# Attention with a bias on one core: the first transposes, copies and casts in another order over the engines, and a planner with other times

## The chip, the cores and the metric

One core of a Trainium2 chip. The metric is the device time of one launch in microseconds (us); the median of the runs counts. The engines: PE (TensorE, matmuls and transposes), DVE (VectorE), ACT (ScalarE), POOL (GpSimd, which here casts a little and issues loads) and SP (which issues transfers). Each takes its own instructions in order; they wait for each other by semaphores.

## The reference

Softmax attention over 4 x 8 heads of 1024 positions and 64 dimensions, with one bias matrix for all heads:

```
scores = q @ k^T / 8 + bias          # 1024 x 1024 per head
attn   = exp(scores - max) / (sum(exp(scores - max)) + 1e-8)
out    = attn @ v                    # float32
```

The kernel leaves the maximum out (the scores are small) and gets the sum as a 65th column of the product with V, which holds ones.

## The kernel before

**Tiling.** Heads go in pairs (16 pairs). The 1024 queries are cut into eight chunks of 128, and these into three passes: A has the chunks 6 and 7, B 3 to 5, C 0 to 2. Pairs go in three groups (0 to 3, 4 to 8, 9 to 15), whose passes run in the order ABC, CAB and BCA. A pass, a pair and a head make a step; a step has two *slots*, so there are 192 slots. A slot is half of the keys against the chunks of the pass and fills two banks of PSUM (512 float32 columns of 128 partitions each) in pass A and three in B and C. Even slots lie in the tile `sx`, odd ones in `sy`.

**What a slot goes through.** PE fills its banks (`s_fill`, L151): the scores come on top of what the banks held. Only the first step of a pass in a group is a *restart*, which clears the banks and adds the bias by matmuls with `btraw`, the bias in bf16. In every later step the product of K (`KA`, `KB`) with Q (`QA`, `QB`) is built so that it takes the scores of the step before away and adds those of the new one; so a bank is never cleared, but PE cannot fill slot s + 2 before slot s has been read. ACT then takes the exponential of the banks into `E` in SBUF (`s_exp`, L202). In marked slots the last bank goes to DVE: L216 takes it out of PSUM (`d_fixed`), and a chain of six further instructions (`d_steps`, L228 to L233) makes the exponential of it by polynomials, into a tile `e`. PE multiplies `E` or `e` with V (`VV`) into `po` (L265); a *unit*, four slots, is divided by its sums and written out by DVE (`evac`, L276 and L277), through three buffers `ob` and SP's queue (L278).

**K and Q** come through POOL's queue in float32 and are cast on the way to bf16 (`kr`, `qr`), are transposed by PE into a PSUM tile `px` of one of two tags, `xa` and `xb` (which the `po` of the units share), and copied by DVE into `KA`, `KB`, `QA` and `QB`; later pairs get some copies by transfers on SP's queue.

**The prologue** (L289 to L487) does the slots 0 to 5 by hand, in the order in which the code is written. The first K, Q and bias chunks come as float32 through the queues of SP and ACT into a part of `E` and are cast by engines, which DVE, ACT and POOL share (L340 to L376 and further); POOL's own loads follow its casts in its queue. The first pair is transposed and scored in halves: `pk` are the transposes of the first head's K, `pq` and `pq_` those of Q, `pk0` the second head's K, `pk1` and `pq1` the second pair. `scores`, `bias_` and `exp_` issue the matmuls of a half and its exponential. A load marked by `after` waits for another's landing.

**The planner** (L490 to L987) emits the rest. It keeps a clock for ACT, PE and DVE and takes whatever could start next by its own costs (L490: 427 for a bank of exponential and so on, in ns). It starts from a state that is written out by hand: when the slots of the prologue end (`act_end`, `fill_end`), when `xa` and `xb` come free (`x_free`), when operands are there (`R`), and when raw K and Q (`raw_at`), V (`v_ready`) and the bias parts land. Its constants set which slots are marked for DVE (`DMIN`, `DTAIL`, the last slots are left out, and `REM`, the work that may be outstanding), how far PE may delay a fill for transposes (`PSL`, `PSU`, `URG`), how many blocks of `E` may wait (`RING`) and behind which slot a load is issued (`G0` to `G5`). Its clock decides only the order; on the chip each instruction waits for what it needs.

Of the kernel before, what the change touches and what calls it, by code (L numbers as in the profile page):

```python
# [9 lines left out]
BF = mybir.dt.bfloat16  # L10
# [6 lines left out]
def kernel(  # L17
# [11 lines left out]
    nc = tc.nc  # L29
    B, H, S, D = q.shape  # L30
    P = 128
    NCH = S // P
# [5 lines left out]
    kf = k.rearrange("b (g t) (p c) d -> (b g) p t (c d)", t=2, p=P)  # L38
# [13 lines left out]
    ps = ctx.enter_context(tc.tile_pool(name="ps", bufs=1, space=bass.MemoryType.PSUM))  # L52

    ident = consts.tile([P, P], BF)
# [4 lines left out]
    btraw = consts.tile([P, NCH, S], BF)  # L59
    KA = consts.tile([P, RP, NCH * P], BF)  # L60
    KB = consts.tile([P, RP, NCH * P], BF)
    QA = consts.tile([P, RP, NCH * P], BF)
    QB = consts.tile([P, RP, NCH * P], BF)
# [61 lines left out]
    raws = {}  # L125
# [11 lines left out]
    def transpose_pe(px, src, c0, n):  # L137
        for c in range(n):
            for t in range(2):
                nc.tensor.transpose(px[t * D:(t + 1) * D, c, :], src[:, t, c0 + c, :], ident[:])  # L140
# [140 lines left out]
    with tc.manual_schedule():  # L281

        def cast(eng, dst, src):
            if eng is nc.scalar:
                eng.copy(dst, src)
            else:
                eng.tensor_copy(dst, src)

        sq0, sk0, sk0b = stage(256), stage(512), stage(512)  # L289
        sc = {6: stage(1024), 7: stage(1024)}  # L290
        sk1, sq1 = stage(1024), stage(256)
# [8 lines left out]
        behind = sp_.dma_start(out=sk0b, in_=kf[0][:, 1])  # L300
# [5 lines left out]
        g, v_, sc_ = nc.gpsimd, nc.vector, nc.vector.tensor_scalar  # L306
# [17 lines left out]
        def q_part(pr, c0, c1, src):  # L324
            return raws[pr, 0][:, :, c0:c1, :], src.rearrange("p (t c d) -> p t c d", t=2, d=D)

        def load_q(pr, c0, c1):
            return g.dma_start(out=raws[pr, 0][:, :, c0:c1, :].rearrange("p t c d -> p t (c d)"),
                               in_=qf[pr][:, :, c0 * D:c1 * D])

        HK = S // 2
        kr0, qr0, kr1, qr1 = raws[0, 1], raws[0, 0], raws[1, 1], raws[1, 0]
        sync = mybir.DependencyInfo(mybir.DependencyClass.Sync, mybir.DependencyReason.SCHED_ONLY)

        def after(later, earlier):

            tc.add_manual_dep(later.ins, earlier.ins.name, sync, reason="pace of the loads")


        cast(g, btraw[:, 6, 5 * P:], sc[6][:, 5 * P:])  # L340
        for pr in (2, 3):
            if pr == 3:
                cast(g, kr1[:, 1].rearrange("p c d -> p (c d)"), sk1[:, 512:])
                load_q(pr, 6, 8)
            x = g.dma_start(out=raws[pr, 1].rearrange("p t c d -> p t (c d)"), in_=kf[pr])
            if pr == 2:
                after(x, behind)
            if pr == 2:
                cast(g, btraw[:, 7, HK:], sc[7][:, HK:])
                load_q(pr, 6, 8)  # L350
        load_q(0, 0, 6)
        g.dma_start(out=btraw[:, 3:6, :], in_=bf_[:, 3:6, :])
        load_v(0)
# [9 lines left out]
        def on(y, lo, hi, inst):  # L363
            for y2, lo2, hi2, x in used:
                if y2 == y and (hi2 <= lo or hi <= lo2):
                    apart(inst, x)
            used.append((y, lo, hi, inst))
            return inst
# [7 lines left out]
        cast(v_, *q_part(0, 6, 8, sq0))  # L376

        pk = [XY[y][:, 1024:1024 + 2 * P].bitcast(BF) for y in range(2)]
        for c in range(NCH):
            on(c // 4, 2, 3, nc.tensor.transpose(pk[c // 4][:D, c % 4 * P:(c % 4 + 1) * P], kr0[:, 0, c, :], ident[:]))  # L380
        pq = ps.tile([P, 2, P], BF, tag="xa", name="px")
        pq_ = ps.tile([P, 2, P], BF, tag="xb", name="px")
        for c in range(2):
            nc.tensor.transpose(pq_[:D, c, :], qr0[:, 0, 6 + c, :], ident[:])
        transpose_pe(pq, qr0, 6, 2)
        on(0, 2, 3, nc.scalar.copy(KA[:D, 0, :HK], pk[0][:D]))
        on(1, 2, 3, v_.tensor_copy(KA[:D, 0, HK:], pk[1][:D]))
        v_.tensor_copy(QB[:D, 0, 6 * P:], pq_[:D].rearrange("p c q -> p (c q)"))
        nc.scalar.copy(btraw[:, 6, :5 * P], sc[6][:, :5 * P])
        sc_(QA[:, 0, 6 * P:], pq.rearrange("p c q -> p (c q)"), sgn[:, :1], None, op0=ALU.mult)  # L390
        sc_(QB[D:, 1, 6 * P:], QA[D:, 0, 6 * P:], -1.0, None, op0=ALU.mult)
# [16 lines left out]
        def exp_(s, y, lo, hi, e):  # L408
            return on(y, lo, hi, nc.scalar.activation(E[:, e * 512:(e + hi - lo) * 512], XY[y][:, lo * 512:hi * 512],
                                                      ACTF.Exp, scale=scale))  # L410

        def fresh():

            return [False] * 3 + [True] + [False] * 3 + [True], [False] * 8

        def add():
            return [False] * 8, [True] * 8
# [6 lines left out]
        for b in range(2):  # L424
            bias_(b, b, 6, 2)
            exp_(0, b, 2, 3, b)
        first, last = fresh()
        for b in range(2):
            bias_(0, b, 6, b)
        cast(v_, kr0[:, 1], sk0b.rearrange("p (c d) -> p c d", d=D))  # L430
        pk0 = ps.tile([P, NCH, P], BF, tag="xa", name="px")
        for c in range(NCH):
            nc.tensor.transpose(pk0[D:, c, :], kr0[:, 1, c, :], ident[:])
        pk0f = pk0.rearrange("p c q -> p (c q)")
        for a in (0, HK):
            v_.tensor_copy(KA[D:, 0, a:a + HK], pk0f[D:, a:a + HK])

        f7, l7 = fresh()
        first, last = f7, l7
# [5 lines left out]
        nc.scalar.copy(btraw[:, 7, :HK], sc[7][:, :HK])  # L445
        for b in range(2):
            exp_(2, 0, b, b + 1, 2 + b)
        first, last = add()
        for b in range(2):
            bias_(b, b, 7, 2)  # L450
            exp_(1, b, 2, 3, 4 + b)
        pk1 = ps.tile([P, NCH, P], BF, tag="xb", name="px")

        def k1_trans(t):
            for c in range(NCH):
                nc.tensor.transpose(pk1[t * D:(t + 1) * D, c, :], kr1[:, t, c, :], ident[:])

        cast(v_, kr1[:, 0], sk1[:, :512].rearrange("p (c d) -> p c d", d=D))
        cast(v_, *q_part(1, 6, 8, sq1))
        v_.tensor_copy(KB[D:, 1, :], pk0f[D:])  # L460
        k1_trans(0)

        first, last = fresh()
        for b in range(2):
            bias_(1, b, 7, b)
        first, last = add()
        scores(1, 0, 1, 7, 0)
        x0 = exp_(3, 1, 0, 1, 6)
        pq1 = ps.tile([P, 2, P], BF, tag="xa", name="px")
        transpose_pe(pq1, qr1, 6, 2)  # L470
        scores(1, 1, 1, 7, 1)
        x1 = exp_(3, 1, 1, 2, 7)
        reads_of[3] = [(0, 1, x0), (1, 2, x1)]
        pass_reads[1] = [(0, 1, x0), (1, 2, x1)]
        fk, fq = pk1.rearrange("p c q -> p (c q)"), pq1.rearrange("p c q -> p (c q)")
        v_.tensor_copy(KB[:D, 1, :], fk[:D])
        v_.tensor_copy(QB[:D, 1, 6 * P:], fq[:D])
        s_fill(4, (0, 1))
        e_pos.update({0: 0, 2: 2, 1: 4, 3: 6, 4: 8, 5: 10})
        s_exp(4, 0, 2)  # L480
# [7 lines left out]


        EXP, EXP0, SEM, E2P, P2E, LATE = 427, 62, 100, 300, 260, 400  # L490
        DMIN, DTAIL, DMAL, RING, PSL, PSU, URG, NEAR, REM = 14, 8, 5200, 38, 60, 150, 24, 3, 5000
        G0, G1, G2, G3, G4, G5 = 18, 5, 12, 56, 6, 8
        act_end = [10800, 11800, 9900, 12000, 13100, 14050]
        fill_end = [0, 0, 0, 0, 12000, 12600]
        t_act, t_pe, t_dve = act_end[-1], 13000, 13800
        bank_end = {s: [fill_end[s]] * 2 for s in range(6)}
        read_end = {s: {0: act_end[s], 1: act_end[s]} for s in range(6)}
        x_free = {"xa": 11800, "xb": 13800}
        R = {("KA", 0): 0, ("KA", 1): 13200, ("QA", 0, "A"): 0, ("QA", 1, "A"): 12000, ("QBt", 0, "A"): 0,
             ("QBb", 2, "A"): 12300, ("KBb", 1): 0, ("KBt", 1): 0, ("KBb", 2): 13900, ("bias", "A"): 0,  # L500
             ("bias", "B"): 20500, ("bias", "C"): 36000}
        raw_at = {(2, 1, 0): 12500, (2, 0, 6): 12900, (3, 0, 6): 13600, (3, 1, 0): 15200, (0, 0, 0): 16300,
                  (1, 0, 0): 23000, (2, 0, 0): 24000, (3, 0, 0): 25000}
        pieces = [(2, 1, 0, 8), (2, 0, 6, 2), (3, 0, 6, 2), (3, 1, 0, 8), (0, 0, 0, 6), (1, 0, 0, 6), (2, 0, 0, 6),
                  (3, 0, 0, 6)]
        v_ready = {0: 22000, 1: 27000, 2: 29000, 3: 31000}
        dma_t = 35000.0
        for pr in range(4, NP):
            pieces += [(pr, 1, 0, NCH), (pr, 0, 0, NCH)]
# [66 lines left out]
        def operands(s):  # L576
# [7 lines left out]
            else:  # L584
                need = [("KBt", pr), ("KBb", pr), ("QBt", pr, c), ("QBb", pr, c)]
            if any(x not in R for x in need):
                return None
            return max(R[x] for x in need)

# [76 lines left out]
        for s in pre_slots:  # L666
            i = s // 2 - 1
# [57 lines left out]
        def tp_done(pr, which, c0, n, px, tag, t):  # L725
# [8 lines left out]
            def done(keys, t2):  # L734
                for k_ in keys:
                    if k_[0][0] == "Q":
                        for x in cls:
                            R[k_ + (x,)] = t2
                    else:
                        R[k_] = t2  # L740

# [209 lines left out]
        while len(act_end) < NS or av_u < NU or dve_q:  # L951
            loads()
            c = []
            a, d, p = act_pick(), dve_pick(), pe_pick()
# [6 lines left out]
            if not c:  # L961
                p = pe_force()
                assert p, (len(fill_end), len(act_end), av_u, pieces[:2])
                c.append((p[0], 2))
            t, who = min(c)
            if who == 0:
                i = len(act_end)
                n = 2 if i in pre_slots else 1
                mark_next(i + n)
                a = act_pick()  # L970
# [7 lines left out]
                t_act = a[2][-1][4]  # L978
                for m in range(n):
                    act_end.append(max(x[4] for x in a[2] if x[0] == i + m))  # L980
            elif who == 1:
                dve_q.remove(d)
                t_dve = t + d[2]
                d[3](t)
            else:
                t_pe = t + p[1]
# [31 lines left out]
```

## Time and profile before

| what | value |
|---|---|
| time, median of 3 runs | 239.59 us (239.46 to 239.92) |
| the profiled execution, its own time | 239.7 us |
| its span, first to last instruction | 237.8 us |
| exponentials on ACT (L204 and L409) | 269 instructions |
| banks of the exponential on DVE (L216) | 40 |
| matmuls with V on PE (L265) | 2048 |
| first exponential of the planned part (L204) starts | 13.23 us |
| first bank taken by DVE (L216) | 23.20 us |
| granted TensorE clock | 0.999 |

A profile line of the timeline has the start and the length in us, the engine, the line of the kernel, the operation, output and input, the shape and how many instructions it merges; in brackets stands how long the engine had been idle before and what ended that. A line of waits has the waiting engine, its tile and line, what it waited for, and the sum in us, the number of times and the longest. `x40` is a count. Consecutive instructions of ACT and DVE overlap by some 0.1 us in their recorded lengths, so that the distance from start to start is the better price.

### The profile page before, as it was taken

To read this page: it belongs to the slowest core of one execution; us is meant where nothing else is said; L and a number is where in the kernel's file an instruction comes from. 1 tells how busy PE (TensorE), PEld (TensorE's weight loads), DVE (VectorE), ACT (ScalarE), POOL (GpSimd) and SP (SyncE) were. 2 spreads that over 40 slices of the span, in tenths; PEclk is the share of its full clock that TensorE was granted. 3 is DMA by queue.
4 is the path that set the end of the run, shared out by engine and by line. 5 is a ranking of instruction groups with operands and counts; after the bars stand their busy time and mean duration, and the time that the engine had idled before them with its cause. 6 is when DMAs were issued, how large, how long until landed. Compare 5 with 4: busy or idle time off the path is not lost.

```text
span 237.8 us, 9441 instructions
## 1 busy us (share of the span) xinstructions
PE 224.2 (94%) x4010; PEld 187.7 (79%) x4010; DVE 220.8 (93%) x461; ACT 225.6 (95%) x275; POOL 57.5 (24%) x82
## 2 busy tenths in 40 slices
PE   7999899999999999999999999999998989989892
PEld 3778788887888889987777888888887777888782
DVE  3686999999989999999999999999999999999993
ACT  4799999999999999999999999999999999999991
POOL 5695502544112224633220332000000000000000
PEclk9999999999999999999999999999999999999999
DMA  7899999999999649999998899312121111111012
GB/s 231 224 136 182 177 195 222 178 189 193 221 211 158 116 93 197 158 183 160 207 209 234 144 135 147 88 44 68 36 69 36 36 34 36 36 55 36 25 48 66
DMA packets 60633, 30.98 MB, mean 130 GB/s; under 512 B 36016, under 2 KB 56624, under 8 KB 60592
## 3 DMA queue, kind: packets, MB, share of 16 engines
q0 software_dynamic: 42272, 13.50, 55.2%
q1 hardware_dynamic: 18176, 16.62, 24.9%
q8 instruction: 31, 0.51, 0.9%
q10 hardware_dynamic: 144, 0.26, 0.5%
q14 instruction: 10, 0.08, 0.1%
HBM read 29.36 MB, written 8.39 MB: 159 GB/s over the span
## 4 chain that ended last, share of the span: by engine, by line
DVE 49%; PE 34%; ACT 7%; issue 7%; DMA 2%; ACTq 0%; DVEq 0%
PE sx L176 9%; PE po L265 8%; PE sy L176 8%; ACT E L204 7%; DVE scr L216 7%; DVE scr L232 7%; DVE e L233 6%; DVE ob L277 6%; DVE scr L231 5%; DVE scr L230 4%; DVE scr L229 4%; PE px L140 4%; DVE scr L228 3%; DVE QA L770 2%; DVE rs L276 2%
## 5 line engine op out<-in xcount | busy, mean ns | idle before, releaser
L204 ACT ACTIVATE E<-sy 128x512 bf16<-128x512 f32 (+2 forms) x151 | 127.9, 906 | 0.2
L204 ACT ACTIVATE E<-sx 128x1024 bf16<-128x1024 f32 (+2 forms) x110 | 115.2, 1065 | 1.5 <-PE sx L176 0.9
L265 PE MATMUL po<-VV,E 128*128 128x65 bf16 x1888 | 84.2, 194 | 2.1 <-DVE ob L277 1.1
L265 PEld LDWEIGHTS <-E 128*128 128x128 bf16 x1888 | 76.0, 98 | 10.3 <-DVE ob L277 2.4
L176 PEld LDWEIGHTS <-KA 128*128 128x128 bf16 x648 | 47.3, 98 | 11.6 <-issue 3.5
L176 PEld LDWEIGHTS <-KB 128*128 128x128 bf16 x600 | 44.0, 98 | 11.7 <-issue 4.6
L134 POOL DMA_DIRECT2D VV<-in_v_dram x32 | 28.8, 905 | 40.9 <-ACT E L204 37.2
L176 PE MATMUL sx<-QA,KA 128*128 128x128 bf16 (+2 forms) x312 | 36.1, 252 | 1.9 <-ACT E L204 1.6
L176 PE MATMUL sx<-QB,KB 128*128 128x128 bf16 (+2 forms) x300 | 35.5, 251 | 2.4 <-ACT E L204 1.7
L176 PE MATMUL sy<-QA,KA 128*128 128x128 bf16 (+2 forms) x312 | 36.0, 252 | 0.4 <-ACT E L204 0.2
L176 PE MATMUL sy<-QB,KB 128*128 128x128 bf16 (+2 forms) x300 | 35.4, 251 | 0.8 <-ACT E L204 0.3
L233 DVE SCALAR_TENSOR_TENSOR e<-scr 128x512 bf16<-128x512 f32 x40 | 27.6, 690 | 1.1
L232 DVE SCALAR_TENSOR_TENSOR scr<-scr 128x512 f32<-128x512 f32 x40 | 27.4, 684 | 0.0
L230 DVE SCALAR_TENSOR_TENSOR scr<-scr 128x512 f32<-128x512 f32 x40 | 27.3, 684 | 0.0
L231 DVE SCALAR_TENSOR_TENSOR scr<-scr 128x512 f32<-128x512 f32 x40 | 27.3, 683 | 0.0
L277 DVE TENSOR_TENSOR ob<-po,rs 128x384 f32<-128x384 f32 (+2 forms) x49 | 24.8, 506 | 2.0 <-DMA out_dram<-ob 0.4
L216 DVE TENSOR_SCALAR scr<-sx 128x512 int32<-128x512 f32 x32 | 21.9, 684 | 1.7 <-ACT E L204 1.5
L131 POOL DMA_DIRECT2D kr<-in_k_dram x12 | 8.5, 705 | 42.2 <-ACT E L204 35.1
L229 DVE TENSOR_SCALAR scr<-scr 128x512 int16<-128x512 int16 x40 | 17.2, 429 | 0.0
L228 DVE TENSOR_SCALAR scr<-scr 128x512 f32<-128x512 uint16 x40 | 17.0, 425 | 0.2
L176 PEld LDWEIGHTS <-btraw 128*128 128x128 bf16 x128 | 11.3, 148 | 1.2 <-issue 0.5
L770 DVE TENSOR_SCALAR QA<-px,sgn 128x1024 bf16<-128x1024 bf16 (+2 forms) x18 | 12.0, 666 | 0.0
(79 smaller groups left out, 167.9 us busy)
## 6 DMA issues: line engine op xcount, KB each, us to landing
out_dram<-ob SPq DMA_DIRECT2D x32, 192.0 KB, 2.8
VV<-in_v_dram POOLq DMA_DIRECT2D x32, 128.0 KB, 7.4
kr<-in_k_dram POOLq DMA_DIRECT2D x14, 256.0 KB, 5.4
KB<-KA SPq DMA_DIRECT2D x24, 128.0 KB, 4.4
qr<-in_q_dram POOLq DMA_DIRECT2D x12, 256.0 KB, 6.7
QB<-qn SPq DMA_DIRECT2D x22, 128.0 KB, 5.8
out_dram<-ob SPq DMA_DIRECT2D x15, 128.0 KB, 4.7
btraw<-in_bias_dram POOLq DMA_DIRECT2D x2, 768.0 KB, 9.0
```

The source lines that it names most:

```text
L134: return [nc.gpsimd.dma_start(out=VV[:, pr % RP, t * NCH:(t + 1) * NCH, :D], in_=vf[pr][:, t].rearrange("p (c d) -> p c d", d=D)) for t in ...
L176: m = nc.tensor.matmul(o, lhsT, rhs, start=restart and i == 0, stop=i == len(todo) - 1 or not restart, skip_group_check=True)
L204: x = nc.scalar.activation(E[:, at:at + (hi - lo) * 512], XY[s % 2][:, lo * 512:hi * 512], ACTF.Exp, scale=scale)
L216: i = nc.vector.tensor_scalar(ys[ch % 2].bitcast(I32), XY[s % 2][:, b * 512:(b + 1) * 512], scale * LOG2E * 65536.0, 127.0 * 65536.0, op0= ...
L228: (340, lambda: v_.tensor_scalar(sf, lo, G / 65536.0, None, op0=ALU.mult)),
L229: (340, lambda: v_.tensor_scalar(sp, hi, 0.0, 128.0, op0=ALU.max, op1=ALU.mult)),
L230: (600, lambda: v_.scalar_tensor_tensor(sb, sf, U2, sf, op0=ALU.add, op1=ALU.mult)),
L231: (600, lambda: v_.scalar_tensor_tensor(y, sf, U1, sf, op0=ALU.add, op1=ALU.mult)),
L232: (600, lambda: v_.scalar_tensor_tensor(sb, sb, V2, sp.bitcast(BF), op0=ALU.add, op1=ALU.mult)),
L233: (650, lambda: v_.scalar_tensor_tensor(e[:], y, V1, sb, op0=ALU.add, op1=ALU.mult)),
L265: nc.tensor.matmul(po[u][:, h - hs[0], c - c0, :], e_block(s, col), VV[:, pr % RP, h * NCH + kc, :], start=first, stop=left[u] == 0, skip_ ...
L277: nc.vector.tensor_tensor(ob[:], acc[:, :, :, :D], rs[:].to_broadcast([P, nh, W, D]), op=ALU.mult)
```

## The change

The prologue gets another order and another sharing, and the planner another starting state and other constants.

- The first K half is copied out of PSUM by DVE instead of ACT, and two transposes of Q move between the two K halves.
- The transposes of the first pair's second K (`pk0`) move ahead of eight bias matmuls, into two PSUM tiles instead of one; the first half of the copy goes to ACT instead of DVE, and the later copy into `KB` is split in two.
- The transposes of the second pair's Q (`pq1`) move ahead of its K's, and the cast of that Q goes from DVE to POOL, ahead of four loads and more in POOL's queue.
- POOL's loads of the pairs 2 and 3: Q of pair 2 goes behind one more cast; the rest keeps its order.
- The planner: other times for the end of the prologue, for tiles, operands and landings; `DTAIL` 9 for 8, `RING` 36 for 38, `PSL` and `PSU` 200 for 60 and 150, `URG` 16 for 24, `REM` 4500 for 5000, and three of the gates of loads.

```diff
--- before.py
+++ after.py
@@ -337,17 +337,17 @@
             tc.add_manual_dep(later.ins, earlier.ins.name, sync, reason="pace of the loads")
 
 
+        def load_k(pr):
+            return g.dma_start(out=raws[pr, 1].rearrange("p t c d -> p t (c d)"), in_=kf[pr])
+
         cast(g, btraw[:, 6, 5 * P:], sc[6][:, 5 * P:])
-        for pr in (2, 3):
-            if pr == 3:
-                cast(g, kr1[:, 1].rearrange("p c d -> p (c d)"), sk1[:, 512:])
-                load_q(pr, 6, 8)
-            x = g.dma_start(out=raws[pr, 1].rearrange("p t c d -> p t (c d)"), in_=kf[pr])
-            if pr == 2:
-                after(x, behind)
-            if pr == 2:
-                cast(g, btraw[:, 7, HK:], sc[7][:, HK:])
-                load_q(pr, 6, 8)
+        after(load_k(2), behind)
+        cast(g, btraw[:, 7, HK:], sc[7][:, HK:])
+        cast(g, *q_part(1, 6, 8, sq1))
+        load_q(2, 6, 8)
+        cast(g, kr1[:, 1].rearrange("p c d -> p (c d)"), sk1[:, 512:])
+        load_q(3, 6, 8)
+        load_k(3)
         load_q(0, 0, 6)
         g.dma_start(out=btraw[:, 3:6, :], in_=bf_[:, 3:6, :])
         load_v(0)
@@ -376,16 +376,17 @@
         cast(v_, *q_part(0, 6, 8, sq0))
 
         pk = [XY[y][:, 1024:1024 + 2 * P].bitcast(BF) for y in range(2)]
+        pq = ps.tile([P, 2, P], BF, tag="xa", name="px")
+        pq_ = ps.tile([P, 2, P], BF, tag="xb", name="px")
         for c in range(NCH):
             on(c // 4, 2, 3, nc.tensor.transpose(pk[c // 4][:D, c % 4 * P:(c % 4 + 1) * P], kr0[:, 0, c, :], ident[:]))
-        pq = ps.tile([P, 2, P], BF, tag="xa", name="px")
-        pq_ = ps.tile([P, 2, P], BF, tag="xb", name="px")
-        for c in range(2):
-            nc.tensor.transpose(pq_[:D, c, :], qr0[:, 0, 6 + c, :], ident[:])
+            if c == 3:
+                for c_ in range(2):
+                    nc.tensor.transpose(pq_[:D, c_, :], qr0[:, 0, 6 + c_, :], ident[:])
         transpose_pe(pq, qr0, 6, 2)
-        on(0, 2, 3, nc.scalar.copy(KA[:D, 0, :HK], pk[0][:D]))
+        on(0, 2, 3, v_.tensor_copy(KA[:D, 0, :HK], pk[0][:D]))
+        v_.tensor_copy(QB[:D, 0, 6 * P:], pq_[:D].rearrange("p c q -> p (c q)"))
         on(1, 2, 3, v_.tensor_copy(KA[:D, 0, HK:], pk[1][:D]))
-        v_.tensor_copy(QB[:D, 0, 6 * P:], pq_[:D].rearrange("p c q -> p (c q)"))
         nc.scalar.copy(btraw[:, 6, :5 * P], sc[6][:, :5 * P])
         sc_(QA[:, 0, 6 * P:], pq.rearrange("p c q -> p (c q)"), sgn[:, :1], None, op0=ALU.mult)
         sc_(QB[D:, 1, 6 * P:], QA[D:, 0, 6 * P:], -1.0, None, op0=ALU.mult)
@@ -424,16 +425,15 @@
         for b in range(2):
             bias_(b, b, 6, 2)
             exp_(0, b, 2, 3, b)
+        cast(v_, kr0[:, 1], sk0b.rearrange("p (c d) -> p c d", d=D))
+        pk0 = [ps.tile([P, HK], BF, tag=t, name="px") for t in ("xa", "xb")]
+        for c in range(NCH):
+            nc.tensor.transpose(pk0[c // 4][D:, c % 4 * P:(c % 4 + 1) * P], kr0[:, 1, c, :], ident[:])
+        nc.scalar.copy(KA[D:, 0, :HK], pk0[0][D:])
+        v_.tensor_copy(KA[D:, 0, HK:], pk0[1][D:])
         first, last = fresh()
         for b in range(2):
             bias_(0, b, 6, b)
-        cast(v_, kr0[:, 1], sk0b.rearrange("p (c d) -> p c d", d=D))
-        pk0 = ps.tile([P, NCH, P], BF, tag="xa", name="px")
-        for c in range(NCH):
-            nc.tensor.transpose(pk0[D:, c, :], kr0[:, 1, c, :], ident[:])
-        pk0f = pk0.rearrange("p c q -> p (c q)")
-        for a in (0, HK):
-            v_.tensor_copy(KA[D:, 0, a:a + HK], pk0f[D:, a:a + HK])
 
         f7, l7 = fresh()
         first, last = f7, l7
@@ -445,36 +445,36 @@
         nc.scalar.copy(btraw[:, 7, :HK], sc[7][:, :HK])
         for b in range(2):
             exp_(2, 0, b, b + 1, 2 + b)
+        cast(v_, kr1[:, 0], sk1[:, :512].rearrange("p (c d) -> p c d", d=D))
+        for i in range(2):
+            v_.tensor_copy(KB[D:, 1, i * HK:(i + 1) * HK], pk0[i][D:])
         first, last = add()
         for b in range(2):
             bias_(b, b, 7, 2)
             exp_(1, b, 2, 3, 4 + b)
+        pq1 = ps.tile([P, 2, P], BF, tag="xa", name="px")
         pk1 = ps.tile([P, NCH, P], BF, tag="xb", name="px")
 
         def k1_trans(t):
             for c in range(NCH):
                 nc.tensor.transpose(pk1[t * D:(t + 1) * D, c, :], kr1[:, t, c, :], ident[:])
 
-        cast(v_, kr1[:, 0], sk1[:, :512].rearrange("p (c d) -> p c d", d=D))
-        cast(v_, *q_part(1, 6, 8, sq1))
-        v_.tensor_copy(KB[D:, 1, :], pk0f[D:])
+
+        transpose_pe(pq1, qr1, 6, 2)
         k1_trans(0)
-
         first, last = fresh()
         for b in range(2):
             bias_(1, b, 7, b)
         first, last = add()
         scores(1, 0, 1, 7, 0)
         x0 = exp_(3, 1, 0, 1, 6)
-        pq1 = ps.tile([P, 2, P], BF, tag="xa", name="px")
-        transpose_pe(pq1, qr1, 6, 2)
         scores(1, 1, 1, 7, 1)
         x1 = exp_(3, 1, 1, 2, 7)
         reads_of[3] = [(0, 1, x0), (1, 2, x1)]
         pass_reads[1] = [(0, 1, x0), (1, 2, x1)]
         fk, fq = pk1.rearrange("p c q -> p (c q)"), pq1.rearrange("p c q -> p (c q)")
+        v_.tensor_copy(QB[:D, 1, 6 * P:], fq[:D])
         v_.tensor_copy(KB[:D, 1, :], fk[:D])
-        v_.tensor_copy(QB[:D, 1, 6 * P:], fq[:D])
         s_fill(4, (0, 1))
         e_pos.update({0: 0, 2: 2, 1: 4, 3: 6, 4: 8, 5: 10})
         s_exp(4, 0, 2)
@@ -488,22 +488,22 @@
 
 
         EXP, EXP0, SEM, E2P, P2E, LATE = 427, 62, 100, 300, 260, 400
-        DMIN, DTAIL, DMAL, RING, PSL, PSU, URG, NEAR, REM = 14, 8, 5200, 38, 60, 150, 24, 3, 5000
-        G0, G1, G2, G3, G4, G5 = 18, 5, 12, 56, 6, 8
-        act_end = [10800, 11800, 9900, 12000, 13100, 14050]
-        fill_end = [0, 0, 0, 0, 12000, 12600]
-        t_act, t_pe, t_dve = act_end[-1], 13000, 13800
+        DMIN, DTAIL, DMAL, RING, PSL, PSU, URG, NEAR, REM = 14, 9, 5200, 36, 200, 200, 16, 3, 4500
+        G0, G1, G2, G3, G4, G5 = 18, 5, 12, 54, 7, 6
+        act_end = [10800, 11800, 9900, 12000, 13400, 14350]
+        fill_end = [0, 0, 0, 0, 12200, 12900]
+        t_act, t_pe, t_dve = act_end[-1], 13100, 14300
         bank_end = {s: [fill_end[s]] * 2 for s in range(6)}
         read_end = {s: {0: act_end[s], 1: act_end[s]} for s in range(6)}
-        x_free = {"xa": 11800, "xb": 13800}
-        R = {("KA", 0): 0, ("KA", 1): 13200, ("QA", 0, "A"): 0, ("QA", 1, "A"): 12000, ("QBt", 0, "A"): 0,
-             ("QBb", 2, "A"): 12300, ("KBb", 1): 0, ("KBt", 1): 0, ("KBb", 2): 13900, ("bias", "A"): 0,
-             ("bias", "B"): 20500, ("bias", "C"): 36000}
-        raw_at = {(2, 1, 0): 12500, (2, 0, 6): 12900, (3, 0, 6): 13600, (3, 1, 0): 15200, (0, 0, 0): 16300,
-                  (1, 0, 0): 23000, (2, 0, 0): 24000, (3, 0, 0): 25000}
+        x_free = {"xa": 12700, "xb": 14300}
+        R = {("KA", 0): 0, ("KA", 1): 13600, ("QA", 0, "A"): 0, ("QA", 1, "A"): 12400, ("QBt", 0, "A"): 0,
+             ("QBb", 2, "A"): 12700, ("KBb", 1): 0, ("KBt", 1): 0, ("KBb", 2): 14300, ("bias", "A"): 0,
+             ("bias", "B"): 21800, ("bias", "C"): 37000}
+        raw_at = {(2, 1, 0): 12000, (2, 0, 6): 13000, (3, 0, 6): 14500, (3, 1, 0): 16000, (0, 0, 0): 18000,
+                  (1, 0, 0): 25500, (2, 0, 0): 27000, (3, 0, 0): 27500}
         pieces = [(2, 1, 0, 8), (2, 0, 6, 2), (3, 0, 6, 2), (3, 1, 0, 8), (0, 0, 0, 6), (1, 0, 0, 6), (2, 0, 0, 6),
                   (3, 0, 0, 6)]
-        v_ready = {0: 22000, 1: 27000, 2: 29000, 3: 31000}
+        v_ready = {0: 23700, 1: 29700, 2: 31600, 3: 33600}
         dma_t = 35000.0
         for pr in range(4, NP):
             pieces += [(pr, 1, 0, NCH), (pr, 0, 0, NCH)]
```

## The prediction

> **What bounds the kernel now.** I read first the shares of the page, then the waits of ScalarE and VectorE, then the timeline of the end.
>
> ```profile
> span 237.8 us, 9441 instructions
> PE 224.2 (94%) x4010; PEld 187.7 (79%) x4010; DVE 220.8 (93%) x461; ACT 225.6 (95%) x275; POOL 57.5 (24%) x82
> DVE 49%; PE 34%; ACT 7%; issue 7%; DMA 2%; ACTq 0%; DVEq 0%
> ```
>
> Three engines are over 93% busy, so shares decide nothing. The chain that ended last runs half through DVE.
>
> ```profile
> DVE scr L216 <- ACT E L204: 1.5, 1, 1.5
> DVE rs L276 <- PE po L265: 0.7, 3, 0.3
> DVE KA L763 <- PE px L140: 0.3, 1, 0.3
> ACT E L204 <- PE sx L176: 0.9, 4, 0.3
> ```
>
> These are the named waits of DVE from 23.2 us on and, in the last line, of ACT from 15 us on. After its first bank of the exponential (L216 at 23.20, which itself waited 1.45) DVE is never idle for more than 0.3 us at a time: up to its last bank the gaps that I find are 0.28, 0.31 and 0.16 (named) and 0.14 and 0.11 (not named), 1.0 in all of 201. ACT shows hardly any idle time, but its busy times overlap: a 1536-wide exp begins 1.35 after the one before, a 1024-wide 0.92, a 512-wide 0.48. Priced so, its exps from the first L204 on fill 213, and they take 219 (13.23 to 232.44): ACT has 6 us of hidden slack and DVE has 1. DVE paces.
>
> ```profile
> 219.58 0.75 ACT L204 ACTIVATE E<-sx 128x512 bf16<-128x512 f32 x1
> 220.16 0.69 DVE L216 TENSOR_SCALAR scr<-sx 128x512 int32<-128x512 f32 x1
> 221.31 1.02 ACT L204 ACTIVATE E<-sx 128x1024 bf16<-128x1024 f32 x1
> 224.14 0.65 ACT L204 ACTIVATE E<-sy 128x512 bf16<-128x512 f32 x1
> 224.17 0.69 DVE L216 TENSOR_SCALAR scr<-sy 128x512 int32<-128x512 f32 x1
> 231.28 1.16 ACT L204 ACTIVATE E<-sy 128x512 bf16<-128x512 f32 x2
> 231.32 0.69 DVE L233 SCALAR_TENSOR_TENSOR e<-scr 128x512 bf16<-128x512 f32 x1
> 232.62 1.32 PE L265 MATMUL po<-VV,E 128*128 128x65 bf16 x32 [0.25 <-DVE ob L277]
> 234.55 0.29 DVE L277 TENSOR_TENSOR ob<-po,rs 128x128 f32<-128x128 f32 x1 [0.40 <-DMA out_dram<-ob]
> ```
>
> The lines at 219.58, 221.31 and 224.14 are ACT at slots 178, 180 and 183; those at 220.16 and 224.17 are DVE taking its banks of 178 and 183, the last. ACT ends at 232.44, DVE's last chain at 232.01: the two are balanced at the end. The last output block ends at 234.84, 2.4 later, because 32 matmuls stand behind that chain and the block waits for its buffer's write.
>
> **The change, part by part.** I compare the order of both programs. Totals are the same: 40 banks on DVE, 472 on ACT, equal matmuls, evacuations and copies. ACT has four exp instructions fewer (two 512 exps begin 0.95 apart in sum, one 1024 0.92, so up to 0.2; ACT does not pace: 0). What differs is the start and which slots give DVE its banks.
>
> *Start, up to DVE's first bank (slot 14 in both).*
> - DVE copies the first half of KA (0.42) and then QB (0.27), from 5.20: first scores at about 5.9 instead of 6.20. ACT, without its 0.58 copy, casts the bias (0.72) from about 5.42, where GpSimd's cast of the same transfer began: 6.14 instead of 6.40. Bias matmuls and first exps are 0.23 earlier.
> - The transposes of the second K half now stand ahead of eight bias matmuls. They need the cast that began at 7.11, when its data landed, and took 0.43. Before, the eight matmuls (7.27 to 7.91) filled that hole. Now PE stands from about 7.1 to 7.6, then does transposes 0.64, bias 0.64, scores 0.6: the next head's scores begin at 9.3, not 9.00, and their exp at 9.75, not 9.43. ACT's added copy (0.58) and its bias cast (0.62) lie between 8.1 and 9.3, under this wait; without it they would cost up to 0.3.
> - The transposes of the second pair's Q move ahead of K's: the exp at 11.95 slips to about 12.45, but the next one then follows at once. ACT enters slot 6 about 0.25 late.
> - GpSimd takes the cast of that Q (256 wide; 384 took 0.50, 512 took 0.61, so about 0.39; DVE's took 0.28). Every load behind it in GpSimd's queue, the pairs 2 and 3, the bias chunks 3 to 5 and V, is issued about 0.4 later. In the old trace the bias landed at about 21.4 and PE used it at 21.49.
> - Slot 14 is now filled before the first of those bias matmuls. Its old fill began at 22.48 though ACT had read slot 12 by 22.19: gain 0.28.
> Sum: +0.25 − 0.28, so 0 for DVE's first bank. Ends: −0.6 (the early gain is kept) and +0.5 (a late load holds the in-order PE).
> The row on GpSimd and VectorE together: the 512-wide DVE cast took 0.43 at 7.11 and 0.63 at 9.31, while GpSimd issued a DMA from 9.01 to 9.72. [...]
>
> *DVE's banks.* Slots with a DVE bank end in 168, 173, 178, 183 before, and in 165, 170, 175, 180 after. The instructions of DVE ahead of the last L216 are almost equal: after it, the old program has eleven chain steps and six evacuations, the new one nine and seven. The two steps are L229 and L230 (0.34 + 0.60), the evacuation is 0.20 + 0.44: the new last L216 comes 0.30 later in DVE's own work. But it belongs to a slot three earlier. Summing the rows, DVE has 0.7 us more to do ahead of a slot than before at slot 18, 1.8 at slot 52, 2.5 at 70, 1.5 at 118, 2.8 at 180; DVE without idle time cannot absorb that, so ACT must run late.
> - DVE reaches the last L216 at 224.17 + 0.30 = 224.47, less the idle time that fuller queues save: 0 to 1.0, I take 0.4. So 224.07.
> - ACT may be ahead of it. L216 came 1.07, 0.62, 0.13, 0.58 and 0.03 after ACT's start of that slot in the last five, mean 0.49; PE cannot fill the bank again before DVE has read it, so much more than 1.07 has no row. ACT starts slot 180 at 223.58, not 221.31.
> - From there ACT took 11.13 (221.31 to 232.44) with one bank given to DVE; the new program gives one too. ACT ends at 234.71.
> - Tail: DVE's last chain now ends well before ACT, its matmuls stand before the last two fills, and 20 matmuls follow the last fill instead of 56. After ACT's end: four matmuls 0.30, reciprocal 0.17, multiply 0.29, hand-overs 0.09 = 0.85, against 2.40 before. The last block ends at 235.56, against 234.84: +0.72.
>
> *The rest of the planner's constants.* K, Q and V loads from pair 9 on and the copies on SP's queue stand in another order. The old trace shows no PE wait for any of them: 0. A late K copy (landing 4.4, the plan allows 5.2) would cost its lateness, at most some 0.5 per case.
>
> Total: span 237.8 + 0.7 = 238.5; the profiled execution took 239.7, 1.9 outside its span: 240.4. The median of the runs is 0.1 below it: **240.3**.
>
> **Rivals.**
> - *Faster: the start gains and carries through.* DVE's first bank comes 0.6 earlier, its 1.0 of idle time vanishes and ACT runs 1.07 ahead: 224.17 + 0.30 − 0.6 − 1.0 − 1.07 + 11.13 + 0.85 = 233.8, −1.1, so 238.6. For it: DVE stood 1.45 before 23.20. Against: the landing at 7.11 sets the start, and all three must be at their ends.
> - *No change: only a rearrangement.* If ACT runs 1.07 ahead and the idle time saved is 0.5, the sum is 234.9: 239.6. That is the reading of equal totals; against it is the lag of 0.03 at the old last bank.
> - *Slower through a late bias.* The bias of chunks 3 to 5 lands at 21.8 or later; PE holds fills 15 to 17 behind it, ACT starves, and DVE, one bank on, idles. It decides from about 22.9 on, where the new order first asks for it; each us behind that costs one. With 1 us: 241.3. [...] For it: the queue slip; against: 1.1 of room.
>
> **How the numbers follow.** Forecast 0.50 (of it 0.42 slower, 0.08 within), late bias 0.17, faster rival 0.20, no change 0.13. What this measurement can tell from no change is about 0.2%, 0.48 us. Slower 0.42 + 0.17 = 0.59, within 0.08 + 0.13 = 0.21, faster 0.20. The forecast's own range takes the ends of start, idle time and lag half way: 239.4 to 241.3. The range for 8 in 10 reaches into the rivals on both sides: 238.6 to 241.5.
>
> **What would show it.** Right: PE idle at 7.1 to 7.6 before L431's transposes; first scores near 5.9; last L216 near 224.1, on slot 180; ACT's last exp near 234.7; DVE idle between evacuations at the end. Wrong: ACT at slot 180 near 221.3, which would mean that DVE does its work sooner than its rows allow or that the lag is longer than any seen; or DVE idle for over 1 us in the middle, which would mean that PE or a load paces.

## The result and the profile after

| what | before | after |
|---|---|---|
| time, median of 4 runs each | 239.69 us (239.46 to 239.92) | 247.98 us (246.98 to 248.42) |
| the profiled execution: time, span | 239.7, 237.8 us | 246.98, 245.0 us |
| first bank taken by DVE (L216) | 23.20 us | 22.40 us |
| last bank taken by DVE (L216) | 224.17 us | 230.14 us |
| granted TensorE clock | 0.999 | 0.982 |

The ratio is 1.0332 [1.0297, 1.0367]: 3.3% slower (the quotient of the two medians in the table is 1.035). The forecast was 240.3 us, its range ended at 241.5. The page of the kernel after, with its shares and the slices of the span (one digit is the busy share of a fortieth of the span, 6.1 us):

```profile
span 245.0 us, 9436 instructions
PE 224.5 (92%) x4010; PEld 187.7 (77%) x4010; DVE 220.7 (90%) x461; ACT 226.1 (92%) x271; POOL 57.6 (23%) x83
PE   7998999999992899999999999999999988798993
DVE  4677999999826999999999999999999999999982
ACT  3899999999992699999999999999999999999993
PEclk9999999999996799999999999999999999999998
```

Work is the same on each engine (DVE 220.7 for 220.8, ACT 226.1 for 225.6, PE 224.5 for 224.2), and the start was 0.80 earlier. The loss is one hole, in the slices 11 to 14, about 61 to 86 us. DVE has it first (8, 2, 6), PE and ACT after it. The waits of the kernel after name it (what waits, for what, sum in us, times, longest):

```profile
ACT E L204 <- PE sx L176: 7.4, 6, 5.8
DVE qn L780 <- DMA QB<-qn: 7.4, 2, 6.8
PE po L265 <- DVE ob L277: 6.7, 5, 4.5
```

The middle line has no counterpart before: DVE waits to *write* `qn`, for the transfers that *read* it. `qn` is the negated Q that L780 leaves in SBUF; two transfers of SP's queue (L782, L786) carry it into `QB`. The pool `qnp` (L48) has two buffers, so a third cast waits until the first one's transfers have landed. The timeline of the kernel after, lines of DVE, SP's queue, PE and ACT:

```profile
64.50 0.42 DVE L780 TENSOR_SCALAR qn<-QA 128x1024 bf16<-128x1024 bf16 x1
65.81 0.55 SPq L782 DMA_DIRECT2D QB<-qn  x1
66.34 0.43 DVE L780 TENSOR_SCALAR qn<-QA 128x1024 bf16<-128x1024 bf16 x1 [0.54 <-DMA QB<-qn]
66.41 0.60 SPq L786 DMA_DIRECT2D QB<-qn  x1
67.88 0.74 DVE L770 TENSOR_SCALAR QA<-px,sgn 128x1024 bf16<-128x1024 bf16 x1
75.46 0.43 DVE L780 TENSOR_SCALAR qn<-QA 128x1024 bf16<-128x1024 bf16 x1 [6.84 <-DMA QB<-qn]
78.51 0.40 PE L265 MATMUL po<-VV,E 128*128 128x65 bf16 x4 [4.51 <-DVE ob L277]
81.06 1.45 ACT L204 ACTIVATE E<-sx 128x1536 bf16<-128x1536 f32 x1 [5.79 <-PE sx L176]
```

Three casts stand within 4 us of DVE's work. The third is ready at 68.6 and begins at 75.46, when the transfers issued at 65.81 and 66.41 have landed: the chain that ended last has the second of them in flight for 8.93 us, from 66.41 to 75.34. DVE is in order, so the exponentials and evacuations behind it wait. PE needs an evacuation (`ob`) before it may write `po`: it stops from 74.00 to 78.51. ACT then has nothing to read until 81.06. In the kernel before, the three casts stand further apart and wait for nothing:

```profile
58.15 0.43 DVE L780 TENSOR_SCALAR qn<-QA 128x1024 bf16<-128x1024 bf16 x1
64.36 0.43 DVE L780 TENSOR_SCALAR qn<-QA 128x1024 bf16<-128x1024 bf16 x1
73.38 0.43 DVE L780 TENSOR_SCALAR qn<-QA 128x1024 bf16<-128x1024 bf16 x1
```

### The profile page after: what moved, and what is told of

Read it like the earlier page. It is cut to its first block, busy times and chain, and to the rows that moved or that the text cites. A ratio compares the mean times of both kernels' runs of the same rounds, so it can differ in the third digit from the quotient of the medians.

```text
span 245.0 us, 9436 instructions
## 1 busy us (share of the span) xinstructions
PE 224.5 (92%) x4010; PEld 187.7 (77%) x4010; DVE 220.7 (90%) x461; ACT 226.1 (92%) x271; POOL 57.6 (23%) x83
## 4 chain that ended last, share of the span: by engine, by line
DVE 44%; PE 32%; ACT 9%; issue 8%; DMA 5%; SPq 0%; ACTq 0%; DVEq 0%
PE sx L176 9%; ACT E L204 9%; PE sy L176 8%; PE po L265 8%; DVE scr L216 6%; DVE scr L231 5%; DVE scr L232 5%; DVE e L233 5%; DVE ob L277 5%; DVE scr L230 5%; PE px L140 4%; DMA QB<-qn 4%; DVE scr L228 3%; DVE scr L229 3%; DMA E<-in_bias_dram 2%
## 5 line engine op out<-in xcount | busy, mean ns | idle before, releaser
L204 ACT ACTIVATE E<-sx 128x1024 bf16<-128x1024 f32 (+2 forms) x125 | 121.8, 1007 | 8.1 <-PE sx L176 7.4
L204 ACT ACTIVATE E<-sy 128x512 bf16<-128x512 f32 (+2 forms) x132 | 119.1, 941 | 2.1 <-PE sy L176 1.8
L265 PE MATMUL po<-VV,E 128*128 128x65 bf16 x1888 | 83.3, 195 | 9.1 <-DVE ob L277 6.7
L176 PE MATMUL sx<-QA,KA 128*128 128x128 bf16 (+2 forms) x312 | 36.6, 255 | 2.1 <-ACT E L204 1.0
L229 DVE TENSOR_SCALAR scr<-scr 128x512 int16<-128x512 int16 x40 | 18.1, 451 | 0.0
L216 DVE TENSOR_SCALAR scr<-sy 128x512 int32<-128x512 f32 x24 | 16.4, 684 | 0.0
L780 DVE TENSOR_SCALAR qn<-QA 128x1024 bf16<-128x1024 bf16 (+2 forms) x14 | 5.7, 406 | 7.7 <-DMA QB<-qn 7.4
L265 PE MATMUL po<-VV,e 128*128 128x65 bf16 x160 | 11.7, 196 | 0.8 <-DVE e L233 0.8
```

What stands on the lines that cost most here:

```text
L176: m = nc.tensor.matmul(o, lhsT, rhs, start=restart and i == 0, stop=i == len(todo) - 1 or not restart, skip_group_check=True)
L204: x = nc.scalar.activation(E[:, at:at + (hi - lo) * 512], XY[s % 2][:, lo * 512:hi * 512], ACTF.Exp, scale=scale)
L216: i = nc.vector.tensor_scalar(ys[ch % 2].bitcast(I32), XY[s % 2][:, b * 512:(b + 1) * 512], scale * LOG2E * 65536.0, 127.0 * 65536.0, op0= ...
L229: (340, lambda: v_.tensor_scalar(sp, hi, 0.0, 128.0, op0=ALU.max, op1=ALU.mult)),
L265: nc.tensor.matmul(po[u][:, h - hs[0], c - c0, :], e_block(s, col), VV[:, pr % RP, h * NCH + kc, :], start=first, stop=left[u] == 0, skip_ ...
```

## The experiments

Ratios are against the kernel before, run on the same chip.

### A third buffer

```diff
-    qnp = ctx.enter_context(tc.tile_pool(name="qnp", bufs=2))
+    qnp = ctx.enter_context(tc.tile_pool(name="qnp", bufs=3))
```

> Theory Q (a lack of qn buffers): in the changed kernel VectorE stood 0.54 and 6.84 us before two instructions of L780, which wait until the transfers that read one of two qn buffers have landed. With three buffers that wait goes: 248.0 - 7.4 = 240.6; the stall also cost some slow matmuls after it, so 239.3 to 240.8, and VectorE has no idle gap over 1 us between its first bank and the last. Rival D (the landing itself is late, the buffer only shows it): PE then waits for the same copies in QB or KB a little later, and 3 us or more stay: over 243.

Measured: 240.02 us, ratio 1.0015 [0.9996, 1.0034], and no wait at L780. One buffer gives back 8 us of the 8.3. The wait is the cause of the slowdown, and all the rest of the change costs no more than 0.34%.

### The constant that brings the casts together

```diff
-... PSL, PSU, URG, NEAR, REM = 14, 9, 5200, 36, 200, 200, 16, 3, 4500
+... PSL, PSU, URG, NEAR, REM = 14, 9, 5200, 36, 200, 200, 24, 3, 4500
```

> Only the planner's URG goes back from 16 to 24. Counted in the program's order, the smallest amount of VectorE work between a qn and the one two later then rises from 3.8 us to 8.4 us (in the kernel before it is 8.3), so theory Q expects no stall with two buffers: 239.3 to 240.8. Rival D, and any theory by which the late part of the new order is at fault, expects no gain from a buffer's distance: 246 to 249.

Measured, with two buffers: 240.1 us, 1.0009 [0.9991, 1.0027], no wait at L780; the three casts begin at 60.48, 65.18 and 68.55. Counting DVE's instructions in program order by their row durations, the work between a cast and the one two later is at least 8.3 us in the kernel before, 3.8 in the kernel after, and 8.4 with `URG` 24. It is also 8.4 with `URG` 16 and the old starting state. The traces bear out three of these: from the start of a cast to the start of the one two later the least is 8.07 us in the kernel before, 8.07 with `URG` 24, and 3.98 in the kernel with the third buffer, in which the changed order runs without the stall. For the fourth there is the count alone and no run. By the count it takes both: the new state and the new `URG`.

### The prologue and the planner apart

The new prologue with the old planner:

```diff
-        DMIN, DTAIL, DMAL, RING, PSL, PSU, URG, NEAR, REM = 14, 9, 5200, 36, 200, 200, 16, 3, 4500
+        DMIN, DTAIL, DMAL, RING, PSL, PSU, URG, NEAR, REM = 14, 8, 5200, 38, 60, 150, 24, 3, 5000
...
-        x_free = {"xa": 12700, "xb": 14300}
+        x_free = {"xa": 11800, "xb": 13800}
...
```

> The new prologue with the planner's old state and constants, so the planned part has the old order. Theory P (the new prologue brings VectorE's first bank forward by 0.8 us, as in the profile of the changed kernel, and VectorE paces from there): 238.9, 238.4 to 239.3. Rival: the forecast's reading, in which the prologue gains nothing: 239.7.

Measured: 240.04 us, 0.9992 [0.9966, 1.0017]: no change. DVE's first bank came at 23.21, not at 22.40. The new prologue alone brings no earlier first bank. With the new planner, which fills slot 14 ahead of the bias matmuls, the first bank came at 22.75 behind the old prologue (the next run) and at 22.89 with `URG` 24, in executions whose second K half was cast at 7.15 and 7.16, as late as in the kernel before (7.11). So the planner's order is worth 0.3 to 0.45 of the 0.80; the rest goes with an execution in which that K half was cast at 6.39. The other half, the old prologue with the new planner:

```diff
-        after(load_k(2), behind)
-        cast(g, btraw[:, 7, HK:], sc[7][:, HK:])
-        cast(g, *q_part(1, 6, 8, sq1))
...
+        for pr in (2, 3):
+            if pr == 3:
...
```

> The old prologue with the planner's new state and constants. Theory Q: the stall belongs to the planned order and stays, and the start is 0.8 later than in the changed kernel: 247 to 250. Rival (the prologue or its later loads make the stall): 239.5 to 241.

Measured: 246.79 us, 1.0289 [1.0252, 1.0326], just under the expected 247. DVE waits at L780 again; from the waits of this kernel:

```profile
DVE qn L780 <- DMA QB<-qn: 5.9, 2, 4.9
```

The stall belongs to the planner's part of the change, whichever prologue stands ahead of it.

### Why the transfers take 9 us

The loads of V for the pairs 5 to 8 go from the gates of the planned part to the prologue, behind the last load there; `qnp` keeps two buffers.

```diff
         g.dma_start(out=btraw[:, :3, :], in_=bf_[:, :3, :])
+        for pr in range(5, 9):
+            load_v(pr)
...
-                for x in load_v(next_v):
+                for x in load_v(next_v) if next_v == 4 or next_v > 8 else []:
```

> The changed kernel, two qn buffers, with the loads of V of the pairs 5 to 8 moved from 45 to 85 us up to behind the last load of the prologue in GpSimd's queue; the order on the other engines stays. If the landing of QB from qn (8.9 us at the median between 60 and 80 us, 4.6 GB/s short of nothing else known) is long because the V loads share the DMA engines, VectorE's wait at the third qn falls from 6.8 to 2 to 5 us and the time to 243 to 246. If the transfer's own length sets it, the wait stays at 5 to 7 and the time at 246 to 249.

Measured: 240.89 us, 1.0045 [1.0019, 1.0071], better than the 243 to 246 that contention was expected to give. No run shows the 4.6 GB/s of the expectation: 128 KB in 8.9 us are 14.7. The issues between 60 and 80 us (count, KB each, median us from issue to landing), first in the kernel after, then in this one:

```profile
VV<-in_v_dram POOLq DMA_DIRECT2D x5, 128.0 KB, 9.2
QB<-qn SPq DMA_DIRECT2D x5, 128.0 KB, 8.9
```

```profile
QB<-qn SPq DMA_DIRECT2D x5, 128.0 KB, 2.3
```

Without V loads beside them the same copies land in 2.3 us instead of 8.9 (those from `KA` into `KB` in 2.9 instead of 7.6). The packets of the queue that carries the V loads took 92% of the time of the 16 DMA engines in that stretch of the kernel after, and 22% here. Only one wait at L780 is left, 1.1 us. So the stall has two factors: casts too close together, 3.8 us of DVE work apart, and transfers that take 8.9 us with the V loads beside them and 2.3 without. With three buffers and the V loads in their place the copies of this stretch still took 7.6 us, and nothing waited for them. In the kernel before, V loads stood beside them too (55 to 75 us, 94%) and they took 5.6. Why it is 8.9 in the kernel after and not 5.6 stays open. With a third buffer as well:

> The changed kernel with both cures: three qn buffers and the V loads of the pairs 5 to 8 moved up. Theory Q with contention (buffers and V loads act on one and the same wait): nothing more is left to gain, the time is that of three buffers alone, 240.0, 239.4 to 240.5. Rival (V loads slow other things in the run as well): under 239.3.

Measured: 240.23 us, 1.0027 [1.0013, 1.0041]. The two cures don't add up: they act on one wait. Moving V is not free, though. On the new prologue with the old planner and two buffers, which has no stall to cure, the same move of V was a miss:

> The new prologue with the planner's old state and constants and the V loads of the pairs 5 to 8 moved up. In the old order VectorE never waited for a qn, so theory Q expects no change against the same without the move: 239.6 to 240.4. Rival: under 239.2.

Measured: 249.98 us, 1.0424 [1.0398, 1.0450]. The waits say why:

```profile
DVE KA L765 <- PE px L140: 8.4, 2, 8.1
PE px L140 <- DMA kr<-in_k_dram: 7.9, 1, 7.9
```

The V loads stand ahead of a later pair's K in POOL's queue, and PE, in order, waits 7.9 us for that K (until 47.66): POOL issued it at 39.40, against 29.22 in the kernel without the move. This is the same kind of loss on another engine.

### Does DVE pace, and has ACT slack?

Two kernels test the premise of the prediction, from the kernel before. The theory that DVE paces ("V") lets added DVE work cost its length and added ACT work nothing or little; its rival has both pace. The added instructions write a spare tile that nothing reads. Six on DVE, ahead of evacuations:

```diff
...
+        if u in (8, 12, 16, 24, 28, 32):
+            nc.vector.scalar_tensor_tensor(spare[:], btraw[:, 6, :512], 1.0, btraw[:, 6, :512], op0=ALU.add, op1=ALU.mult)
```

> The kernel before with six more VectorE instructions (128x512 float32 results of a length like L230's, 0.60 us from start to start), one ahead of each of six evacuations in the middle of the run; nothing reads them. Theory V (VectorE paces from its first bank on, with 1.0 us of idle time): 239.8 + 3.6 - up to 1.0 = 242.4 to 243.4. Rival B (the three engines are balanced by their shares and the gaps of each absorb it): 240 to 241.5.

Measured: 242.53 us, 1.0113 [1.0093, 1.0133]: +2.7 us for 3.6 us of work, inside V's range. And six on ACT, behind exponentials:

```diff
...
+        if lo == 0 and s in (40, 60, 80, 110, 130, 150):
+            nc.scalar.copy(spare[:], btraw[:, 6, :512])
```

> The kernel before with six more ScalarE copies of 128x512 (0.5 to 0.6 us each, about 3.3 in all) behind the exponentials of six slots from 40 to 150; nothing reads them. Theory V (ScalarE has some 6 us of hidden waiting): each is absorbed in part, 240 to 241.5. Rival (ScalarE, 95% busy, paces as much as VectorE): 242.5 to 243.3.

Measured: 242.12 us, 1.0086 [1.0055, 1.0116]: +2.1 us for 3.3 us of work, between both expectations. The run isn't clean: DVE waits once for `qn` here too (in the lines of this kernel, L783 is the cast of L780):

```profile
130.63 0.43 DVE L783 TENSOR_SCALAR qn<-QA 128x1024 bf16<-128x1024 bf16 x1 [0.85 <-DMA QB<-qn]
```

The profiled execution took 242.70, 3.0 more than the kernel before; two of the other three took 241.62, 1.9 more. If the whole of the 0.85 reached the end, the added ACT work itself costs between 1.2 us (2.1 − 0.85) and 2.2 (3.0 − 0.85), more than a third of its length. So ACT's 6 us of idle time don't hide it. By the distances from start to start the idle stretches of ACT in the profile before are at most 1.0 each; why added work doesn't fill them is not shown. Per us of added work DVE costs 0.75 (0.62 to 0.89 by the interval) and ACT 0.62 (0.40 to 0.84): that DVE has the higher price is not shown.

### Candidates

The numbers behind these were guesses at a better order, each with three `qn` buffers. The first takes the new prologue, the old starting state, and other constants (`DMIN` 15, `DMAL` 7000, `RING` 36, `URG` 20, `REM` 5500, three gates as after):

> The new prologue, three qn buffers, the planner's old hand-written state and a set of constants (DMIN 15, DTAIL 8, RING 36, PSL 60, PSU 150, URG 20, REM 5500, DMAL 7000) that gives VectorE its first bank in slot 18 and its last in a place where the work of ScalarE behind it is 1.8 us shorter than in the kernel before. By theory V the hand-over of the last bank sets the end: 238 to 239.3. Rival: a later first bank costs what the later ones gain, 239.5 to 240.5.

Measured: 242.87 us, 1.0133 [1.0105, 1.0162], above both expectations. DVE stands idle early, ahead of the copy of transposes that PE makes late:

```profile
DVE QB L769 <- PE px L140: 6.1, 3, 4.9
```

PE itself waited only 0.63 there for raw Q. The first bank, which fills this stretch in the kernel before, comes later in DVE's order (29.67 instead of 23.20), so that the copy is the next instruction there.

The second changes one time of the old planner, after which it gives DVE 39 banks instead of 40; once with the new prologue, once with the old:

```diff
-             ("bias", "B"): 20500, ("bias", "C"): 36000}
+             ("bias", "B"): 21100, ("bias", "C"): 36000}
```

> The new prologue, three qn buffers, the planner's old state and constants but for the landing of bias B, 21100 for 20500. The order that follows gives VectorE 39 banks, not 40: 3.9 us less on VectorE (0.69 + 0.34 + 0.34 + 0.60 + 0.61 + 0.63 + 0.70) and 0.45 more on ScalarE. If VectorE alone paced: 236 to 237.5. From the two runs with added work, in which 3.6 us on VectorE cost 2.7 and 3.3 on ScalarE cost 2.1, about 240 - 2.9 + 0.3: 236.8 to 238.4. Rival (ScalarE and PE set the end as soon as VectorE is lighter): 239 to 240.3.

> The same planner and three qn buffers with the old prologue: 39 banks on VectorE as well. If the two prologues are worth the same, as the run with the new prologue and the old planner says, the same time within 0.4 us of the other; if the new one gains where VectorE has room, 0.4 to 0.8 slower than the other.

Measured: 245.61 us, 1.0251 [1.0236, 1.0267], and 246.47 us, 1.0291 [1.0271, 1.0312]. Both miss by 6 us, and again not at the banks. The stretch from 40 to 60 us (busy time of PE, PEld, DVE, ACT and POOL), before and with the new prologue:

```profile
40.00:60.00 20.00, 19.79 (x347) 16.29 (x347) 19.59 (x39) 19.75 (x21) 9.82 (x12) 1.00 1.29 192
```

```profile
40.00:60.00 20.00, 16.66 (x266) 12.87 (x264) 13.83 (x27) 16.58 (x16) 7.82 (x10) 1.00 1.26 196
```

DVE lacks 5.8 us there. PE's timeline of the kernel with the new prologue shows part of what is late:

```profile
51.17 0.64 PE L140 MATMUL px<-ident,qr 128*64 128x128 bf16 x16 [1.11 <-DMA qr<-in_q_dram]
57.36 0.64 PE L140 MATMUL px<-ident,kr 128*64 128x128 bf16 x16 [1.57 <-DMA kr<-in_k_dram]
```

The two waits are 2.7 us; the rest of the 5.8 is not broken down. One of the planner's own times, set 0.6 us later, reorders the plan so that transposes are asked for ahead of the landing of their operands. Between these two the new prologue is 0.86 us faster (in the profile of the old one PE also ran at half its clock for at least 3.36 us, in the other it didn't), with the old planner there is no difference (0.9992 with an interval of 0.5%), and with the new planner the kernel with the new prologue is the slower one (1.0332 against 1.0289, intervals that overlap). What the new prologue is worth by itself stays open. No kernel here beats the one before.

## Why the prediction was wrong

**The step that failed** is the last of the change: "K, Q and V loads from pair 9 on and the copies on SP's queue stand in another order. The old trace shows no PE wait for any of them: 0. A late K copy (landing 4.4, the plan allows 5.2) would cost its lateness, at most some 0.5 per case." In its place the runs show 7.4 us of waits at L780, and a third buffer takes 8 us away (247.98 to 240.02). It failed in three ways:
- It asked who *consumes* the copies, PE. The waiting engine was the one that *produces* them: DVE, for a free buffer. A buffer count of two is a dependency that no row shows as long as the casts are far apart.
- It gave no price to a distance that shrank. The page before has QB<-qn at 5.8 us from issue to landing. Against 3.8 us of DVE work between a cast and the one two later, that alone is 2 us of wait, more than the +0.72 that the whole forecast comes to. And the landing is no constant: in the stretch of the stall the copies took 8.9, with V loads beside them, and 2.3 without.
- Its bound, 0.5, was a lateness against the planner's allowance of 5.2. The planner's clock doesn't know the buffers of `qnp` at all, so nothing limits that term.

**The other steps** can be read from the third-buffer kernel, which is the changed kernel without the stall. Its end (timeline, ACT at slot 180 and after, DVE's last bank, the last exponential and the last block):

```profile
222.51 0.74 ACT L204 ACTIVATE E<-sx 128x512 bf16<-128x512 f32 x1
223.12 0.68 DVE L216 TENSOR_SCALAR scr<-sx 128x512 int32<-128x512 f32 x1
...
233.05 1.12 ACT L204 ACTIVATE E<-sy 128x512 bf16<-128x512 f32 x2
...
234.76 0.29 DVE L277 TENSOR_TENSOR ob<-po,rs 128x128 f32<-128x128 f32 x1
```

| term | forecast | third buffer | after |
|---|---|---|---|
| first L216 | 23.20 | 22.56 | 22.40 |
| last L216 (slot 180) | 224.07 | 223.12 | 230.14 |
| its lag behind ACT | 0.49 | 0.61 | 0.62 |
| ACT from there to its end | 11.13 | 11.66 | 11.66 |
| tail after ACT | 0.85 | 0.88 | 0.90 |
| last block ends | 235.56 | 235.05 | 242.08 |

- *Start: forecast 0, measured −0.64 and −0.80.* The hole before L431's transposes didn't come: in the two executions the cast of the second K half began at 6.39 and 6.69 instead of 7.11, since its data had landed earlier. Two others with this prologue began it at 7.03 and 7.16; with 7.03 (the old planner) PE did stand ahead of L431's transposes, for 0.28. The term for slot 14 (−0.28) came, as 0.3 to 0.45; the other part of the earlier start is luck of the landing. First scores stood at 5.86 (third buffer) as forecast, 5.53 after.
- *GpSimd's new cast.* It took 0.40 (estimate 0.39). It began at 9.16, after 0.47 of idle time that the trace puts down to the landing of its data; DVE's cast of 8.74 ended at 9.17 (8.74 + 0.43). In the third-buffer kernel it began at 9.49, again after 0.47, and DVE's cast ended at 9.51 (9.08 + 0.43). That one of these casts held the other up is not shown. The bias chunks were issued at 12.90 instead of 12.88, at 13.23 with the third buffer, and at 13.20 and 13.21 in the two executions with the late K half: 0.3 late, where the prediction had 0.4. In the kernel after PE waits for no bias load, and with that the late-bias rival fell.
- *DVE's banks and the tail: right in mechanism.* Slot 180 is the last, DVE's reciprocals at the end wait (0.57, 0.68, 1.03), and the sum errs by −0.5 in all. That it errs by no more is partly luck: the earlier start (−0.64), a shorter stretch to the last bank (−0.31) and a longer lag (−0.12) are partly given back by ACT's last stretch (+0.53).
- *"DVE paces, ACT has 6 us of hidden slack": half wrong.* Added DVE work cost 0.75 of its length, as pacing would have it, but added ACT work cost over a third of its own, so ACT's slack was not free.

Without the stall the forecast of 240.3 stands 0.3 above the measured 240.02. And the falsifier was named: DVE idle for over 1 us in the middle. It fired, but "that PE or a load paces" was the wrong reading of it.

## What to carry to other kernels

When a change reorders issue, check for each pool with few buffers how much work now lies between a write and the one that reuses its buffer, and hold it against the landing time of the transfer that reads it: no row of the old trace shows that margin as a wait. Price a wait on every engine that touches the tile, the producer too, and remember that an in-order producer passes it to all that stands behind: here DVE's 6.84 us became 4.51 on PE and 5.79 on ACT. A planner that doesn't model a resource moves its conflicts at will; one constant of 0.6 us or one threshold cost 6 to 8 us here.

## What the runs showed of the hardware

**Half speed after a wait.** In the kernel after, PE stood from 74.00 to 78.51, and then ran at half its clock. Windows of that stretch (start to end, length, busy us and counts of PE, PEld, DVE, ACT and POOL, granted clock, DMA share, GB/s):

```profile
74.00:76.00 2.00, 0.00 (x0) 0.00 (x0) 0.54 (x2) 1.27 (x2) 0.00 (x0) 0.98 2.31 162
76.00:78.00 2.00, 0.00 (x0) 0.00 (x0) 1.97 (x6) 0.00 (x0) 0.00 (x0) 0.50 1.41 119
78.00:80.00 2.00, 1.25 (x8) 0.75 (x9) 1.97 (x4) 0.00 (x0) 0.00 (x0) 0.50 0.44 118
80.00:82.00 2.00, 1.56 (x19) 1.23 (x19) 1.93 (x6) 0.94 (x1) 0.00 (x0) 0.50 0.01 4
82.00:84.00 2.00, 2.00 (x43) 1.78 (x42) 1.97 (x4) 1.37 (x2) 1.20 (x2) 0.81 0.31 98
```

A fill of six matmuls took 1.33 there (at 81.71) instead of 0.83. Shorter windows give the ends: the mean is 0.94 over 75.50 to 76.00 and 0.74 over 82.50 to 83.00, so the clock was 0.50 from 75.94 to 82.76, which is 6.82 us. In the same way it was 0.50 from 78.89 to 82.30 (3.41 us) in the old prologue with the new planner, from 44.58 to 51.42 (6.84 us) in the kernel that waits 7.9 us for K, and from 56.64 to 60.00 at least (3.36 us) in the old prologue with 39 banks. 3.41 us is about half of the two long lengths; what sets them is not shown, nor how long a stop makes the clock fall. It fell 1.94 us after PE had stopped in the kernel after, 1.91 after it (from 54.73) in the old prologue with 39 banks, and 4.79 after it (from 39.79) in the kernel that waits for K. In the old prologue with the new planner a stop of 3.01 us, to 77.07, left the clock at 1.00, and it fell at 78.89, in the next stop, of 1.19 us.

**A copy's landing time is not its own.** The same 128 KB transfer between two SBUF tiles landed in 2.3 us with no V loads beside it and in 5.6 to 8.9 us with them (medians of five copies in a stretch of 20 us). And the landing that set the start, that of the second K half, let its cast begin between 6.39 and 7.16 in executions of one prologue, so that the start of one profile is known only within some 0.8 us.
